# Up projection of a gated MLP: two running sums that shared one two-bank PSUM tile get a tile each

## The chip, the cores and the metric

The kernel runs on one core of a Trainium2 chip. TensorE (PE) multiplies matrices and writes to PSUM, VectorE (DVE) and ScalarE (ACT) do element-wise work and read PSUM, GpSimd (POOL) and SyncE (SP) here issue DMA transfers. PSUM has eight banks of 2 KB per partition; 512 float32 numbers fill one bank. The metric is the device time of the kernel in microseconds; lower is better. Several runs are taken and their median is given.

## The reference

One encoder layer on 512 tokens of 2048 channels, in float32: a norm, an input projection, a convolution group and a neighbourhood-attention group, an output projection with residual, and then the gated MLP in which the change lies:

```python
xn = rms_norm(x, ffn_norm_g[l])
up = jnp.einsum("bsd,df->bsf", xn, w_up[l])          # 2048 -> 2 * 5632
up = depthwise_conv(up, ffn_dw_w[l], ffn_dw_b[l])    # width 3 over positions
gate, val = jnp.split(up, 2, axis=-1)
x = x + jnp.einsum("bsf,fd->bsd", jax.nn.silu(gate) * val, w_down[l])
```

A last norm follows.

## The kernel before

The work is laid out with channels on the 128 partitions and the 512 tokens along the free dimension. The up projection is done in 44 tiles (`NF`); tile `f` makes 128 gate channels and the 128 value channels that go with them, for all tokens, in `up(f, done)` (L647). `hidden` (L707) scales the result, runs the width-3 convolution (`conv3`, L694), applies the activation and multiplies; all but the last four tiles are stored to DRAM.

Each tile is a 2 x 2 block product: gate and value rows by even and odd chunks of the input channels, times even and odd chunks by the first and second half of the tokens (`H` = 256). It is computed with seven block products in place of eight, in the order `TURN` = 3, 2, 4, 5, 1, 0, 6. The combinations of the input that they need are made once and kept (`comb`, `halves`, L543). The combinations of the weights are made for each tile: some by a DMA that adds while it writes (`summed`, L603, its POOL transfer on L605), some by DVE (L615, L617).

To keep float32 accuracy, every operand is split into a high and a low part. A unit of weights (128 x 1024) is loaded to `raw` (L110), ACT makes its high part `whi` (L115), and DVE makes the rest, `wlo` (L116). `weights()` (L151) makes units three products ahead of their use; there are four buffers for each of `whi` and `wlo` and nine for `raw`. Sums by DMA are started eight products ahead.

A block product has eight steps. In `product` (L649) a step is one matmul of the high weights with 512 columns (L656; 256 columns of high input and 256 of low input) and one of the low weights with 256 columns (L659). Product 2 does it in three matmuls of 256 columns (`mm3`, L125). So a PSUM bank holds two halves that have yet to be added: `folded` (L668) copies the right half to SBUF on ACT (L669) and adds the left half on DVE (L670).

Five banks hold running sums of one tile: `pa`, `pe`, `pd_`, `pb` and `pc_`. They are allocated once, before the loop over tiles. `pa` is begun by product 3, and products 4 and 1 are added to it. Between these, `copied` (L664) copies it on ACT (L666) to other banks, from which these go on:

- after product 3: `pd_` is a copy of `pa`, to which product 5 is added; folded, it is the first token half of the gate
- after product 4: `pe` is a copy of `pa`, to which product 0 is added; folded, it is the first token half of the value, before `w` is added
- after product 1: `pb` is a copy of `pa`, to which product 6 is added; folded, it is the second token half of the gate
- `pa` itself after product 1, folded, is the second token half of the value, before `w` is added
- `pc_` takes product 2, and goes to both value halves as `w` (L677, L689)

`pd_`, `pb` and `pc_` are PSUM tiles of one bank each. `pe` and `pa` are the two banks of one PSUM tile, `ea` (tag "sc"), and one `folded(by, ea)` reads both of them after product 0. The attention stage uses the tags "sc" and "po" earlier, and the down projection uses them again afterwards (`four`, L761). Three matmuls on L645 begin `pe`, `pd_` and `pb` once, before the first tile.

The program is written in order; a scheduler gives each engine its queue, and each engine then works through its own queue in order. Waits between engines are put in from the reads and writes of tiles. `pin` keeps a matmul behind the one written before it; where the list `tight` isn't empty, the first matmul of each product and the first of each step of `mm3` are pinned. Here `tight` is filled in tile 0 after product 3, and emptied after the last tile. `done` is called after each product: it issues transfers that prepare the down projection's weights (`sum_ahead`, L175; two POOL transfers per tile, L181 and L184), and in the last tile it starts reading the stored tiles back (L748).

Of the kernel before, what the change touches and what calls it, by code (L numbers as in the profile page):

```python
# [10 lines left out]
F32 = mybir.dt.float32  # L11
# [5 lines left out]
P = 128  # L17
D = 2048
S = 512
# [51 lines left out]
def layer(ctx: ExitStack, tc: tile.TileContext, xT, w_in, w_out, w_up, w_down, par, tab, g3, out):  # L71
# [7 lines left out]
    psa = ctx.enter_context(tc.tile_pool(name="psa", bufs=1, space=bass.MemoryType.PSUM))  # L79

    @contextmanager
    def shifted(by):

        at = tc.cur_priority
        tc.cur_priority = max(at + by, 0)
        yield
        tc.cur_priority = at + (tc.cur_priority - max(at + by, 0))

    def t2(name, dt=F32):
        return tp.tile([P, S], dt, tag="t2k", name=name)  # L90
# [32 lines left out]
    tight = []  # L123

    def mm3(ps, w, wk, mh, ml, start, stop, more=False):  # L125
        hi, lo = w[:2]
        a = slice(wk * P, (wk + 1) * P)
        i = nc.tensor.matmul(ps, hi[:, a], mh, start=start, stop=False, skip_group_check=more)  # L128
        if tight:
            pin(i)  # L130
        nc.tensor.matmul(ps, hi[:, a], ml, start=False, stop=False, skip_group_check=more)  # L131
        return nc.tensor.matmul(ps, lo[:, a], mh, start=False, stop=stop, skip_group_check=more)  # L132
# [4 lines left out]
    def tick(behind):  # L137
        for todo in (steps, asteps):
            while todo:
                try:  # L140
                    with tc.issue_after(behind.ins):
                        next(todo[0])
                    break
                except StopIteration:
                    todo.pop(0)
# [5 lines left out]
    def weights():  # L151
        at = weights.at
        weights.at += 1
        for i in range(at, min(at + 1 + FAR, len(plan))):
            if i in sums:
                sums.pop(i)()
        while len(made) < min(at + 1 + AHEAD, len(plan)):
            made.append(plan[len(made)]())
        return made[at]
# [478 lines left out]
    where.append(1)  # L638
    steps.append(stats2())

    ea = psa.tile([P, 2, S], F32, tag="sc", name="pu")
    pd_, pb, pc_ = (psm.tile([P, S], F32, tag="mm", name="pu") for _ in range(3))
    pe, pa = ea[:, 0], ea[:, 1]
    for x in (pe, pd_, pb):
        nc.tensor.matmul(x, comb[3][0][:, :P], comb[3][0], start=True, stop=True)  # L645

    def up(f, done):  # L647

        def product(c, ps, more):  # L649
            hi, lo = wt = weights()  # L650
            for k in range(U):
                m, w = comb[c][k], slice(k * P, (k + 1) * P)
                if c == 2:
                    i = mm3(ps[:, :H], wt, k, m[:, :H], m[:, H:], k == 0, k == U - 1)
                    continue
                i = nc.tensor.matmul(ps, hi[:, w], m, start=k == 0 and not more, stop=False, skip_group_check=more)  # L656
                if k == 0 and tight:
                    pin(i)
                i = nc.tensor.matmul(ps[:, :H], lo[:, w], m[:, :H], start=False, stop=k == U - 1,  # L659
                                     skip_group_check=more)  # L660
            tick(i)
            done(TURN.index(c), i)

        def copied(to, ps):  # L664
            with shifted(-100):
                nc.scalar.activation(to, ps, AF.Copy)  # L666

        def folded(to, ps):  # L668
            nc.scalar.activation(to, ps[..., H:], AF.Copy)  # L669
            add(to, to, ps[..., :H])  # L670

        product(3, pa, False)
        tight[:] = [1]
        copied(pd_, pa)
        product(2, pc_, False)
        w = t2("w")[:, :H]
        nc.scalar.activation(w, pc_[:, :H], AF.Copy)  # L677
        product(4, pa, True)
        copied(pe, pa)
        product(5, pd_, True)  # L680
        g = t2("g")
        folded(g[:, :H], pd_)
        product(1, pa, True)
        copied(pb, pa)
        product(0, pe, True)
        v = t2("vl")
        by = v.rearrange("p (i t) -> p i t", i=2)
        folded(by, ea)
        add(by, by, w.unsqueeze(1).broadcast_to([P, 2, H]))  # L689
        product(6, pb, True)  # L690
        folded(g[:, H:], pb)
        return g, v
# [14 lines left out]
    def hidden(f, done):  # L707
        g, v = up(f, done)
        nc.vector.tensor_mul(g, g, rstd2[0])
        nc.vector.tensor_mul(v, v, rstd2[0])  # L710
        g, v = conv3(g, f), conv3(v, NF + f)
        nc.scalar.activation(g, g, AF.Silu)
        nc.vector.tensor_mul(g, g, v)
        if f < NF - KEEP:
            nc.sync.dma_start(hd[f], g)
        else:
            hs[f] = g
# [236 lines left out]
```

## Time and profile before

| | before |
|---|---|
| runs | 2113.78, 2118.54, 2118.21 us |
| median | 2118.21 us |
| the profiled execution's own time | 2115.08 us |
| its span, first to last instruction | 2113.1 us |
| mean granted TensorE clock | 0.996 |
| up projection's matmuls | from 706.5 to 1678.2 us |

The profile records one execution. Its page gives the busy time of each engine, the span in slices, the chain that ended last, and the costliest groups of instructions by source line. Views of the trace list who waited for whom (in order: engine, line and what it waited for, us in total, times, the longest), the instructions of a stretch in order of time (start, duration, engine, line, operation, result and operands, and in square brackets the idle time before it and what ended it), and the busy time of each engine in chosen stretches. Matmuls are pipelined, so their records overlap: the distance between two starts is what one costs. PEld is the loading of weights into the array, which overlaps matmuls. A name such as `pu` stands for all five PSUM sums of the up projection, `vl` and `g` for the value and gate results, `xc` for the input combinations.

### The profile page before, as it was taken

Reading aid. Unit: us, or ns where it says so; the run is one execution under the profiler, and the core shown is the slowest. Engines: PE = TensorE matmul, PEld = TensorE weight load, DVE = VectorE, ACT = ScalarE, POOL = GpSimd, SP = SyncE. Lnnn points to the kernel's source line nnn. Section 1 sums busy time; section 2 is a strip of 40 time slices with the busy share of each in tenths; the row PEclk is TensorE's granted clock in tenths of the full one; section 3 lists DMA queues with packets and bytes.
Section 4 is the critical chain, followed back from the end, with each engine's and each line's share of the span. In section 5 each row is a group of like instructions: output and inputs, shape, how many; then the busy total and the mean of one; then the engine's idle time right before and its main releaser. Section 6 shows DMA issues by size and latency. Waiting matters only on the chain.

```text
span 2113.1 us, 28490 instructions
## 1 busy us (share of the span) xinstructions
PE 2011.4 (95%) x10511; PEld 1682.2 (80%) x10511; DVE 1603.5 (76%) x2267; ACT 1091.4 (52%) x1680; POOL 230.1 (11%) x318
## 2 busy tenths in 40 slices
PE   8999999999999899999999999999999899999997
PEld 6888888877887787878878788787878788888886
DVE  7986796685658787877778777787877798887765
ACT  6144424456436565555555555555555554554553
POOL 0111111110011111111111111111110210000000
PEclk9999999999999999999999999999999999999999
DMA  6777677668578788888988888889886786666663
GB/s 245 178 219 190 160 189 187 181 181 266 162 180 217 175 218 241 206 246 219 236 231 225 231 213 240 227 219 253 206 238 166 262 305 215 212 211 197 190 204 116
DMA packets 141755, 446.81 MB, mean 211 GB/s; under 512 B 15920, under 2 KB 24112, under 8 KB 140208
## 3 DMA queue, kind: packets, MB, share of 16 engines
q1 hardware_dynamic: 98352, 293.99, 41.2%
q0 software_dynamic: 43264, 151.01, 34.3%
q8 instruction: 82, 1.34, 0.2%
q14 instruction: 57, 0.47, 0.1%
HBM read 426.07 MB, written 111.15 MB: 254 GB/s over the span
## 4 chain that ended last, share of the span: by engine, by line
PE 66%; issue 24%; ACT 5%; DVE 3%; DMA 2%; POOL 0%; SPq 0%; DVEq 0%; POOLq 0%; ACTq 0%
PE pu L656 21%; PE pu L659 9%; PE pj L128 6%; PE pj L132 6%; PE pj L131 6%; ACT whi L115 3%; PE po L128 3%; PE po L132 3%; PE po L131 3%; PE pu L128 2%; PE pu L131 2%; PE pu L132 2%; DVE vl L670 1%; ACT pu L666 1%; PE po L454 1%
## 5 line engine op out<-in xcount | busy, mean ns | idle before, releaser
L115 ACT ACTIVATE whi<-raw 128x1024 fp32r<-128x1024 f32 x574 | 607.1, 1058 | 886.4 <-PE pu L656 331.2
L116 DVE TENSOR_TENSOR wlo<-raw,whi 128x1024 fp32r<-128x1024 f32 x574 | 697.3, 1221 | 398.8 <-ACT whi L115 375.8
L656 PE MATMUL pu<-xc,whi 128*128 128x512 f32 x2112 | 758.8, 402 | 73.6 <-ACT pu L666 66.7
L659 PE MATMUL pu<-xc,wlo 128*128 128x256 f32 x2112 | 591.8, 280 | 0.0
L656 PEld LDWEIGHTS pu<-xc,whi 128*128 128x128 f32 x2112 | 396.7, 188 | 192.6 <-ACT pu L666 80.7
L659 PEld LDWEIGHTS pu<-xc,wlo 128*128 128x128 f32 x2112 | 398.9, 189 | 0.3 <-issue 0.2
L128 PE MATMUL pj<-xh,whi 128*128 128x512 f32 x640 | 253.4, 397 | 8.3 <-ACT whi L115 8.3
L132 PE MATMUL pj<-xh,wlo 128*128 128x512 f32 x640 | 250.4, 392 | 0.6 <-DVE wlo L116 0.6
L131 PE MATMUL pj<-xl,whi 128*128 128x512 f32 x640 | 250.7, 392 | 0.0
L776 PE MATMUL pd<-whi,ho 128*128 128x512 f32 x616 | 240.4, 391 | 1.6 <-ACT ho L737 1.6
L778 PE MATMUL pd<-whi,ho 128*128 128x512 f32 x616 | 240.2, 390 | 0.6 <-DVE ho L738 0.6
L777 PE MATMUL pd<-wlo,ho 128*128 128x512 f32 x616 | 240.4, 390 | 0.0
L328 DVE SCALAR_TENSOR_TENSOR y<-ch,prm,y 128x507 f32<-128x507 f32 (+14 forms) x240 | 169.7, 739 | 3.3
L128 PEld LDWEIGHTS pj<-xh,whi 128*128 128x128 f32 x640 | 120.7, 189 | 36.5 <-ACT whi L115 9.6
L132 PEld LDWEIGHTS pj<-xh,wlo 128*128 128x128 f32 x640 | 120.5, 188 | 27.9 <-DVE wlo L116 2.1
L131 PEld LDWEIGHTS pj<-xl,whi 128*128 128x128 f32 x640 | 120.7, 189 | 24.6 <-issue 0.7
L776 PEld LDWEIGHTS pd<-whi,ho 128*128 128x128 f32 x616 | 115.9, 188 | 26.1 <-ACT ho L737 1.9
L778 PEld LDWEIGHTS pd<-whi,ho 128*128 128x128 f32 x616 | 116.1, 188 | 25.2 <-DVE ho L738 1.1
L184 POOL DMA_DIRECT2D ws<-in_w_down x88 | 79.5, 903 | 516.5 <-DMA ws<-ws 271.6
L777 PEld LDWEIGHTS pd<-wlo,ho 128*128 128x128 f32 x616 | 116.1, 188 | 24.4 <-DVE wlo L116 0.3
L605 POOL DMA_DIRECT2D raw<-in_w_up x88 | 82.5, 937 | 486.7 <-DMA raw<-in_w_up 284.0
L128 PE MATMUL pu<-xc,whi 128*128 128x256 f32 x352 | 100.3, 285 | 0.0
(170 smaller groups left out, 2485.0 us busy)
## 6 DMA issues: line engine op xcount, KB each, us to landing
raw<-in_w_up SPq DMA_DIRECT2D x220, 512.0 KB, 5.8
ws<-in_w_down POOLq DMA_DIRECT2D x132, 512.0 KB, 6.2
raw<-in_w_up POOLq DMA_DIRECT2D x88, 512.0 KB, 8.0
raw<-ws SPq DMA_DIRECT2D x88, 512.0 KB, 4.3
raw<-in_w_in SPq DMA_DIRECT2D x80, 512.0 KB, 5.2
raw<-in_w_down SPq DMA_DIRECT2D x66, 512.0 KB, 4.4
ws<-ws POOLq DMA_DIRECT2D x44, 512.0 KB, 7.1
raw<-in_w_out SPq DMA_DIRECT2D x32, 512.0 KB, 5.0
```

The source lines that it names most:

```text
L115: i = nc.scalar.activation(hi[:, :n], raw[:, :n], AF.Copy)
L116: j = nc.vector.tensor_sub(lo[:, :n], raw[:, :n], hi[:, :n].bitcast(F32))
L128: i = nc.tensor.matmul(ps, hi[:, a], mh, start=start, stop=False, skip_group_check=more)
L131: nc.tensor.matmul(ps, hi[:, a], ml, start=False, stop=False, skip_group_check=more)
L132: return nc.tensor.matmul(ps, lo[:, a], mh, start=False, stop=stop, skip_group_check=more)
L328: nc.vector.scalar_tensor_tensor(y[:, a:b], h[:, a + j - PAD:b + j - PAD], prm[:, o + j:o + j + 1], y[:, a:b], op0=ALU.mult, op1=ALU.add)
L605: nc.gpsimd.dma_start(a[c], w_up[f, q2], accum_op=ALU.add)
L656: i = nc.tensor.matmul(ps, hi[:, w], m, start=k == 0 and not more, stop=False, skip_group_check=more)
L659: i = nc.tensor.matmul(ps[:, :H], lo[:, w], m[:, :H], start=False, stop=k == U - 1, skip_group_check=more)
L776: nc.tensor.matmul(ps[i], h[:, t], wh[:, d], start=start and not more, stop=False, skip_group_check=more)
L777: nc.tensor.matmul(ps[i], h[:, t], wl[:, d], start=False, stop=False, skip_group_check=more)
L778: return nc.tensor.matmul(ps[i], h[:, tl], wh[:, d], start=False, stop=stop, skip_group_check=more)
```

## The change

`pa` becomes the first bank of the "sc" tile, whose second bank isn't used; `pe` becomes a tile of its own, in the one-bank slot "po". The joint fold of both value halves becomes two folds of 256 columns, `pa`'s first, both still written after product 0. `tight` stays empty through tile 0: no matmul is pinned there, nor is the first one of tile 1's product 3; from tile 1's product 2 on all is pinned as before.

```diff
-    ea = psa.tile([P, 2, S], F32, tag="sc", name="pu")
+    pa = psa.tile([P, 2, S], F32, tag="sc", name="pu")[:, 0]
+    pe = psa.tile([P, S], F32, tag="po", name="pu")
     pd_, pb, pc_ = (psm.tile([P, S], F32, tag="mm", name="pu") for _ in range(3))
-    pe, pa = ea[:, 0], ea[:, 1]
     for x in (pe, pd_, pb):
         nc.tensor.matmul(x, comb[3][0][:, :P], comb[3][0], start=True, stop=True)
...
         product(3, pa, False)
-        tight[:] = [1]
+        tight[:] = [1] * (f > 0)
         copied(pd_, pa)
...
         product(0, pe, True)
         v = t2("vl")
         by = v.rearrange("p (i t) -> p i t", i=2)
-        folded(by, ea)
+        folded(by[:, 1], pa)
+        folded(by[:, 0], pe)
         add(by, by, w.unsqueeze(1).broadcast_to([P, 2, H]))
```

## The prediction

> **What bounds the kernel now.** I read the page's totals first, then the list of waits, then the timeline of one steady tile of the up projection on each engine.
>
> ```profile
> span 2113.1 us, 28490 instructions
> PE 2011.4 (95%) x10511; PEld 1682.2 (80%) x10511; DVE 1603.5 (76%) x2267; ACT 1091.4 (52%) x1680; POOL 230.1 (11%) x318
> ```
>
> TensorE (PE) works 95% of the span, so only what makes PE wait, or a new engine overtaking it, moves the end. The list of waits names two PE waits that come once per tile f (44 tiles):
>
> ```profile
> ACT whi L115 <- PE pu L656: 331.2, 218, 3.1
> PEld pu L656 <- ACT pu L666: 80.7, 44, 1.8
> PE pu L656 <- ACT pu L666: 66.7, 44, 1.5
> PEld pu L656 <- DVE vl L670: 17.4, 43, 0.4
> ```
>
> 44 waits on a PSUM copy (L666) and 43 on the value fold's add (L670). ACT's weight split (L115) in turn waits for PE, and no DMA stands in ACT's list for this stage: weights are ahead. The steady tile on PE:
>
> ```profile
> 1081.32 0.50 PE L656 MATMUL pu<-xc,whi 128*128 128x512 f32 x1 [1.52 <-ACT pu L666]
> ...
> 1093.10 0.40 PE L656 MATMUL pu<-xc,whi 128*128 128x512 f32 x1
> 1093.33 0.28 PE L659 MATMUL pu<-xc,wlo 128*128 128x256 f32 x1
> 1093.45 0.40 PE L656 MATMUL pu<-xc,whi 128*128 128x512 f32 x1
> ...
> 1095.93 0.40 PE L656 MATMUL pu<-xc,whi 128*128 128x512 f32 x1
> ...
> 1101.47 0.28 PE L659 MATMUL pu<-xc,wlo 128*128 128x256 f32 x1
> 1103.26 0.50 PE L656 MATMUL pu<-xc,whi 128*128 128x512 f32 x1 [1.52 <-ACT pu L666]
> 1103.60 0.28 PE L659 MATMUL pu<-xc,wlo 128*128 128x256 f32 x1
> ...
> 1108.90 0.28 PE L659 MATMUL pu<-xc,wlo 128*128 128x256 f32 x1
> 1109.24 0.50 PE L656 MATMUL pu<-xc,whi 128*128 128x512 f32 x1
> 1109.57 0.28 PE L659 MATMUL pu<-xc,wlo 128*128 128x256 f32 x1
> ```
>
> The two waiting rows are product 0 of neighbouring tiles: the period is 1103.26 - 1081.32 = 21.94 us. Product 4 starts at 1093.10 and product 5 at 1095.93, so a product that waits for nothing takes 2.83; within it a 512-column matmul is followed after 0.23 and a 256-column one after 0.12. Product 0 starts 1.79 after the last matmul of product 1 (1101.47), 1.67 more than 0.12, and its first matmul takes 0.34 instead of 0.23: **1.77 us lost**, 0.1 of it a restart cost. Product 3 of the next tile starts at 1109.24, 0.34 after 1108.90, and loses 0.22 + 0.10 = **0.32 us**. Together 2.09 of 21.94.
>
> **Why PE waits there.** The other engines over the same stretch:
>
> ```profile
> 1096.98 0.58 ACT L666 ACTIVATE pu<-pu 128x512 f32<-128x512 f32 x1
> ...
> 1101.67 1.06 ACT L115 ACTIVATE whi<-raw 128x1024 fp32r<-128x1024 f32 x1 [1.50 <-PE pu L656]
> 1102.63 0.58 ACT L666 ACTIVATE pu<-pu 128x512 f32<-128x512 f32 x1
> ...
> 1107.23 0.58 ACT L669 ACTIVATE vl<-pu 128x512 f32<-128x512 f32 x1
> ```
> ```profile
> 1104.01 1.23 DVE L615 TENSOR_TENSOR raw<-raw 128x1024 f32<-128x1024 f32 x1
> 1107.36 1.23 DVE L116 TENSOR_TENSOR wlo<-raw,whi 128x1024 fp32r<-128x1024 f32 x1 [2.12 <-ACT whi L115]
> 1108.50 0.68 DVE L670 TENSOR_TENSOR vl<-vl,pu 128x512 f32<-128x512 f32 x1
> ...
> 1111.17 0.68 DVE L710 TENSOR_TENSOR vl<-vl,rstd 128x512 f32<-128x512 f32 x1
> ```
>
> Product 0 adds to `pe`, which was copied out of `pa` at 1096.98 and was ready at 1097.56. It starts only when the next copy (`pb` out of `pa`, 1102.63 to 1103.21) has ended. That copy neither reads nor writes `pe`; it reads the other bank of the same tile. Product 5, whose `pd_` is a tile of its own, starts at 1095.93, with no wait, 1.05 us before the copy of that moment (1096.98). So the wait comes from sharing a tile. ACT makes it longer because the copy stands behind a weight split (1101.67). The 0.32 us has the same root: product 3 overwrites `pa`, whose only fold is the joint one, and its add ends at 1109.18.
>
> The rule of the Trainium skill, "PSUM — Partial Sum Buffer", section "PSUM bank collisions raise a hardware error", is that different engines must be kept apart by bank and quadrant; different banks ran clean together. By it the wait guards nothing and can go; the row of product 5 agrees.
>
> **The change part by part.**
>
> *`pe` to a tile of its own (bank "po").* Removes the 1.77 us in all 44 tiles: 44 x 1.77 = 77.9 us. The copy `pb` out of `pa` stays as late as now: 1.74 us after the last matmul of product 1 starts (1101.47 to 1103.21). It is next needed by product 6, one product (2.83) after product 0's start: 2.83 + 0.12 - 1.74 = 1.2 us to spare. If that cover went, product 6 would take over the wait. Bounds: 0 (the wait is something else) to 77.9. I take 77.9, since all 44 waits name this copy.
>
> *Value halves folded singly.* The half in `pa` no longer waits for product 0. Its ACT copy can follow L666 at 1103.2 and its add can follow L615 at 1105.2, four microseconds before product 3 needs `pa`: 43 x 0.32 = 13.8 us. Bounds 0 to 13.8; I take 13.8. The cost of two small operations in place of one:
>
> ```profile
> L669 ACT ACTIVATE g<-pu x88: 361/366/374, 727.8 to 1679.9; 128x256 f32<-128x256 f32 x88
> L670 DVE TENSOR_TENSOR g<-g,pu x88: 409/414/415, 729.0 to 1681.3; 128x256 f32<-128x256 f32 x88
> ...
> L669 ACT ACTIVATE vl<-pu x44: 577/581/595, 735.1 to 1680.5; 128x512 f32<-128x512 f32 x44
> L670 DVE TENSOR_TENSOR vl<-vl,pu x44: 678/680/681, 736.4 to 1682.7; 128x512 f32<-128x512 f32 x44
> ```
>
> In this tile's view (min/median/max ns), ACT gets 2 x 366 - 581 = 151 ns more a tile and DVE 2 x 414 - 680 = 148 ns. I cost both at nothing, because the engines have room in the shorter period:
>
> ```profile
> 600.00:700.00 100.00, 99.94 (x463) 80.37 (x462) 75.54 (x137) 57.06 (x104) 13.01 (x17) 1.00 0.86 211
> ...
> 1085.30:1107.23 21.93, 20.35 (x122) 17.56 (x121) 16.93 (x20) 12.12 (x18) 3.25 (x4) 1.00 0.87 239
> ```
>
> (Columns: stretch, its length, busy time of PE, PEld, DVE, ACT, POOL, then clock, DMA share, GB/s.) DVE would have 16.93 + 0.15 = 17.08 of 21.94 - 2.09 = 19.85 us, 86%; ACT 62%. Without cover they would cost 44 x 0.15 = 6.6 us each. The first row, of the output projection, shows PE 99.94% busy at clock 1.00, so a fuller PE need not lose clock.
>
> *Order free in the first tile.* `tight` stays empty in tile 0, so its products and the first product of tile 1 aren't held behind the matmul before them. The place where that can matter:
>
> ```profile
> 713.58 0.79 PE L656 MATMUL pu<-xc,whi 128*128 128x512 f32 x1 [3.25 <-DVE xc L547]
> ```
> ```profile
> 713.50:716.00 2.50, 2.42 (x11) 2.33 (x11) 1.36 (x5) 1.93 (x6) 0.00 (x0) 0.50 0.94 140
> 716.00:718.00 2.00, 2.00 (x10) 2.00 (x10) 1.75 (x9) 1.15 (x2) 0.00 (x0) 0.50 1.08 216
> 718.00:720.00 2.00, 2.00 (x14) 2.00 (x14) 1.76 (x5) 0.00 (x0) 0.00 (x0) 0.71 0.13 32
> ```
>
> PE waits 3.25 us for the last operand of product 3. Product 2 is next, and needs the same operands only for its eighth step; seven steps of three 256-column matmuls at 0.12 are 2.5 us and could fill that wait. Bounds: a loss of 1.0 (product 2 no longer covers the copy `pd_` out of `pa`, 0.4 to 1.0 us after product 3) to a gain of 2.5 plus the slow clock that follows the wait, 4.5 us at 0.50 and 2.0 at 0.71, which is 2.25 + 0.58 = 2.8 of lost work, together 5.3. I take 2.5. By the Trainium skill's "TensorE: Matmul & The Clock Gate", section "What's actually happening", about 3.4 us of idleness halves the clock. The rows after the 3.25 us wait agree, and the steady tile's 1.52 us waits do not trigger it (clock 1.00). By that rule a filled wait keeps the clock and the first tile gives 5.3, with a total 2.8 us lower.
>
> *What comes next.* The tightest feed is product 1's summed weight: it is loaded, then a second load is added on top by POOL.
>
> ```profile
> 1091.71 1.42 SPq L110 DMA_DIRECT2D raw<-in_w_up  x2
> ```
> ```profile
> 1099.29 0.86 POOL L605 DMA_DIRECT2D raw<-in_w_up  x1 [10.12 <-DMA raw<-in_w_up]
> ```
> ```profile
> 1112.29 1.06 ACT L115 ACTIVATE whi<-raw 128x1024 fp32r<-128x1024 f32 x1 [1.86 <-issue]
> ```
>
> The load starts when DVE frees a buffer, and lands 7.6 us later; the adding transfer takes about as long, so its sum is there at about 1106.9. By the order of the weights the split at 1112.29, right after product 3, is the one that reads it: 5.4 us to spare, 3.3 in the shorter tile. So I charge nothing.
>
> *Sum.* The profiled execution took 2115.1 us, 2.0 more than its span. 2115.1 - 77.9 - 13.8 - 2.5 = 2020.9. The median of the runs (2118.2) is 3.1 above the profiled execution, so **2024 us** is my forecast for the median.
>
> **The rivals.**
>
> 1. *DMA takes part of it back.* The DMA share of 0.87 over 21.93 us is 19.1 us of packets, 96% of a 19.85 us tile. For it: in this row the queues are the fullest resource after PE. Against it: two queues overlap (a share of 1.08 stands above), and they are fed in bursts behind DVE, not late for ACT now. If packets stretch by a tenth when nothing is idle, the tile is 21.0 and the gain 44 x 0.94 = 41 us: 2118.2 - 41 - 2.5, about 2075.
>
> 2. *The change doesn't do what it says.* If product 0 waited for the copy for another reason than the tile, only 13.8 + 2.5 remain: 2102. Against it: product 5's row.
>
> 3. *Slower: the `pa` fold's add falls behind in DVE's queue.* Product 3 of the next tile waits for it. DVE's run from 1107.36 to 1111.17 is unbroken; if the scheduler placed this add last in that run, it would end 2.15 us after product 6 (1108.90 + 0.12). Product 3 would then lose about 2.25 instead of 0.32, which cancels the 1.77. The kernel is slower from 2.09 us of lateness on. Two weight subtractions (L116, 1.23 each) ahead of it as well make 2.4 more: 2118.2 + 43 x (2.25 + 2.4 - 2.09) - 2.5 = 2226. Against it: the add is ready before that run starts, with DVE idle from 1105.24 to 1107.36.
>
> 4. *The joint wait only.* If product 3 keeps its 0.32 because both folds are issued together, 2038.
>
> **How the numbers follow.** Forecast 0.70 (first-tile bounds and a run spread of a few us make its own range 2014 to 2033); rival 4 0.08; rival 1 0.14; rival 2 0.03; rival 3 0.05. The range 2014 to 2062 holds the forecast, rival 4 and the milder third of rival 1, which is 0.8 with some tail left below. A measurement tells 0.3% (6.4 us) from no change. Faster: 0.70 + 0.08 + 0.14 + 0.02 of rival 2 = 0.94; within 0.3%: 0.02, from rivals 2 and 3; slower: 0.04.
>
> **What would show it.** Right: the 44 PE waits on L666 vanish and product 0 starts 0.12 us after product 1's last matmul, with L666 running beside it; no PE wait on L670; the tile's period is 19.85; the first tile has no 3.25 us wait on L547. Wrong: PE waits on L666 now stand at product 6; ACT's L115 waits on DMA (rival 1); PE waits on L670 over 2 us (rival 3); or the period stays near 21.9 (rival 2).

## The result and the profile after

| | before | after |
|---|---|---|
| median of the runs | 2117.07 us (4 runs, 2113.78 to 2118.54) | 2020.44 us (4 runs, 2018.15 to 2021.26) |
| the profiled execution's own time | 2115.08 us | 2021.06 us |
| its span | 2113.1 us | 2019.1 us |

The ratio is 0.9544, with a 95% interval from 0.9527 to 0.9560: the kernel is 4.6% faster. The forecast was 2024 us, with a range from 2014 to 2062.

The totals of the page after, and its chain that ended last:

```profile
span 2019.1 us, 28450 instructions
## 1 busy us (share of the span) xinstructions
PE 1990.3 (99%) x10511; PEld 1682.7 (83%) x10511; DVE 1608.5 (80%) x2311; ACT 1104.1 (55%) x1724; POOL 230.2 (11%) x318
...
PE 97%; ACT 1%; DMA 1%; DVE 1%; issue 0%; SPq 0%; POOLq 0%; POOL 0%; DVEq 0%
```

PE has the same 10511 matmuls in 94.0 us less. ACT and DVE each have 44 instructions more: the single folds. Both PE waits of the up projection are gone from the list of waits. This is PE around product 0, product 6 and the next product 3 of a steady tile:

```profile
1004.77 0.28 PE L659 MATMUL pu<-xc,wlo 128*128 128x256 f32 x1
1004.88 0.40 PE L656 MATMUL pu<-xc,whi 128*128 128x512 f32 x1
...
1007.60 0.28 PE L659 MATMUL pu<-xc,wlo 128*128 128x256 f32 x1
1007.72 0.40 PE L656 MATMUL pu<-xc,whi 128*128 128x512 f32 x1
...
1010.42 0.28 PE L659 MATMUL pu<-xc,wlo 128*128 128x256 f32 x1
1010.53 0.40 PE L656 MATMUL pu<-xc,whi 128*128 128x512 f32 x1
```

Product 0 starts at 1004.88, 0.11 us after the last matmul of product 1 (1.79 before). Product 6 starts at 1007.72 and product 3 of the next tile at 1010.53, both without a gap; in the steady tiles no first matmul takes 0.50 any more. ACT in that time:

```profile
1004.97 1.06 ACT L115 ACTIVATE whi<-raw 128x1024 fp32r<-128x1024 f32 x1 [1.50 <-PE pu L656]
1005.94 0.58 ACT L666 ACTIVATE pu<-pu 128x512 f32<-128x512 f32 x1
1006.45 0.37 ACT L669 ACTIVATE vl<-pu 128x256 f32<-128x256 f32 x1
1007.92 0.39 ACT L669 ACTIVATE vl<-pu 128x256 f32<-128x256 f32 x1 [1.10 <-PE pu L659]
```

The copy still stands behind the weight split, as late as before. But now it runs beside product 0, and ends at 1006.52, 1.20 us before product 6 needs it. `pa`'s fold follows at once; `pe`'s comes when product 0 has ended. The stretch of one tile, with the columns as above (length, PE, PEld, DVE, ACT, POOL, clock, DMA share, GB/s):

```profile
1000.00:1019.85 19.85, 19.85 (x122) 17.61 (x122) 17.26 (x22) 12.42 (x19) 3.24 (x4) 1.00 0.97 254
```

PE is busy all the time. Where the 94.0 us of span came from, by the starts of products in both traces:

| part | before | after | difference |
|---|---|---|---|
| start of the span to the first product of tile 0 | 707.22 | 710.10 | +2.88 |
| from there to product 2 of tile 1 | 32.75 | 25.52 | -7.23 |
| 42 tiles, product 2 to product 2 | 42 x 21.897 | 42 x 19.840 | -86.41 |
| from the last product 2 to the down projection | 20.45 | 18.78 | -1.67 |
| down projection to the end | 433.01 | 431.44 | -1.57 |

The first row is no effect of the change. Execution e7 below does the same work there and reached the first product at 705.79; the two part between 500 and 510 us, where the clock is 0.66 and PE busy for 5.74 us in the kernel after, against 1.00 and 7.95 in e7. The last row holds a fall of the clock too: just behind the up stage, from 1680 to 1685 us, it is 0.67 in the kernel before, and the kernel after has no such fall there (1.00 from 1590 to 1600); whether that belongs to the change isn't shown. So the comparisons that follow use the length of the up stage alone, from its first product to the first matmul of the down projection (before 972.87 us, after 877.56, a gain of 95.3).

### The profile page after: what moved, and what is told of

It is laid out like the page before. It is cut to its first block, busy times and chain, and to the rows that moved or that the text cites. A ratio compares the mean times of both kernels' runs of the same rounds, so it can differ in the third digit from the quotient of the medians.

```text
span 2019.1 us, 28450 instructions
## 1 busy us (share of the span) xinstructions
PE 1990.3 (99%) x10511; PEld 1682.7 (83%) x10511; DVE 1608.5 (80%) x2311; ACT 1104.1 (55%) x1724; POOL 230.2 (11%) x318
## 4 chain that ended last, share of the span: by engine, by line
PE 97%; ACT 1%; DMA 1%; DVE 1%; issue 0%; SPq 0%; POOLq 0%; POOL 0%; DVEq 0%
PE pu L656 25%; PE pu L659 12%; PE pj L128 7%; PE pj L132 7%; PE pd L778 7%; PE pd L779 7%; PE pd L777 7%; PE pj L131 7%; PE po L128 3%; PE po L131 3%; PE po L132 3%; PE pu L128 2%; PE pu L131 2%; PE pu L132 2%; PE po L454 1%; PE sc L414 1%
## 5 line engine op out<-in xcount | busy, mean ns | idle before, releaser
L656 PE MATMUL pu<-xc,whi 128*128 128x512 f32 x2112 | 748.8, 399 | 0.0
L128 PE MATMUL pj<-xh,whi 128*128 128x512 f32 x640 | 254.4, 399 | 8.0 <-ACT whi L115 8.0
L128 PEld LDWEIGHTS pj<-xh,whi 128*128 128x128 f32 x640 | 121.3, 189 | 36.3 <-ACT whi L115 9.4
L131 PEld LDWEIGHTS pj<-xl,whi 128*128 128x128 f32 x640 | 121.2, 189 | 24.7 <-issue 0.7
L128 PE MATMUL pu<-xc,whi 128*128 128x256 f32 x352 | 99.7, 283 | 0.5 <-ACT xc L546 0.5
```

## The experiments

Each was timed against the kernel before, run again beside it (medians 2116.43 us for e1 to e4, 2117.03 for e5 to e7, 2116.77 for e8 and e9). The stage lengths come from one profiled execution each.

| kernel | median us | ratio to before, 95% | up stage us | steady tile us |
|---|---|---|---|---|
| e1, after, tile 0 pinned | 2025.97 | 0.9573 (0.9560 to 0.9586) | 882.87 | 19.84 |
| e2, before, tile 0 free | 2111.98 | 0.9981 (0.9972 to 0.9991) | 968.42 | 21.91 |
| e3, before, halves folded singly | 2169.03 | 1.0251 (1.0238 to 1.0264) | 1025.46 | 23.10 |
| e4, after, `pa`'s fold late | 2022.20 | 0.9555 (0.9541 to 0.9570) | 877.55 | 19.84 |
| e5, after, `pd_` shares instead | 2260.93 | 1.0681 (1.0660 to 1.0701) | 1099.26 | 25.20 |
| e6, before, copy ahead of the split | 2068.78 | 0.9770 (0.9752 to 0.9788) | 926.88 | 20.83 |
| e7, after, one more transfer a tile | 2018.54 | 0.9535 (0.9516 to 0.9555) | 877.57 | 19.84 |
| e8, after, two more | 2019.60 | 0.9538 (0.9522 to 0.9555) | 877.50 | 19.84 |
| e9, after, four more | 2093.92 | 0.9892 (0.9874 to 0.9910) | 954.73 | 19.84, then 19.8 to 24.7 |

### e1 and e2: what the free first tile is worth

```diff
 e1, from the kernel after
-        tight[:] = [1] * (f > 0)
+        tight[:] = [1]
 e2, from the kernel before
-        tight[:] = [1]
+        tight[:] = [1] * (f > 0)
```

> The changed kernel with tile 0 pinned as before. Theory: filling the 3.25 us wait of tile 0 is worth 5.2 us (tile 0 took 32.75 us from its first product to tile 1's product 2 before, 25.52 after, and 2.06 of the difference is what every tile gains), half of it by the clock that no longer falls. So 2020.4 + 5.2, about 2025.6 us, with the wait on L547 of about 3.2 us and a clock near 0.5 behind it back again, and a steady tile of 19.84 us. Rival: the time saved in tile 0 is lost again at its edges (the stage started 2.9 us later after the change): 2020 to 2022 us.

> The kernel before with only the first tile's order freed. Theory: 2117 - 5.2, about 2112 us, the 44 waits of product 0 on L666 unchanged and the steady tile still 21.9 us. Rival: the two parts need each other, or tile 0's gain is lost at its edges: 2116 to 2118 us.

Putting the pins back costs 882.87 - 877.56 = 5.3 us of the stage; freeing the tile alone gives 972.87 - 968.42 = 4.5 us, and 2116.43 to 2111.98 in the medians. Within a microsecond the two parts add, and the saving isn't lost at the edges. In e1, PE in tile 0, first its timeline and then its stretches:

```profile
716.07 0.80 PE L656 MATMUL pu<-xc,whi 128*128 128x512 f32 x1 [3.25 <-DVE xc L547]
```
```profile
716.00:718.50 2.50, 2.44 (x11) 2.34 (x11) 1.35 (x5) 1.92 (x6) 0.00 (x0) 0.50 0.92 197
718.50:721.00 2.50, 2.50 (x13) 2.50 (x13) 2.25 (x9) 1.15 (x2) 0.00 (x0) 0.50 0.92 178
```

and the same place in the kernel after:

```profile
716.24 0.39 PE L128 MATMUL pu<-xc,whi 128*128 128x256 f32 x1 [0.52 <-ACT xc L546]
```
```profile
716.00:718.50 2.50, 2.26 (x16) 2.13 (x17) 2.35 (x9) 2.49 (x9) 0.00 (x0) 1.00 0.95 166
718.50:721.00 2.50, 2.50 (x16) 2.18 (x15) 2.36 (x9) 1.86 (x3) 0.00 (x0) 1.00 0.96 175
```

With the pins, PE waits 3.25 us and then works at clock 0.50. Without them, product 2 (L128) fills the wait, 0.52 us is left, and the clock stays at 1.00. So the gain has two halves: the wait, and the slow clock behind it.

The pins of the later tiles do nothing here. With `tight` left empty throughout, the compiled program is the same as the kernel after, instruction for instruction, so it has no run of its own.

### e3 and e5: does the wait belong to the shared tile?

e3 is the kernel before with the new folding, `pe` and `pa` still in one tile. e5 is the kernel after with `pd_` put in `pa`'s tile; `pe` keeps its own.

```diff
 e3, from the kernel before
-        folded(by, ea)
+        folded(by[:, 1], pa)
+        folded(by[:, 0], pe)
 e5, from the kernel after
-    pa = psa.tile([P, 2, S], F32, tag="sc", name="pu")[:, 0]
+    ad = psa.tile([P, 2, S], F32, tag="sc", name="pu")
+    pd_, pa = ad[:, 0], ad[:, 1]
     pe = psa.tile([P, S], F32, tag="po", name="pu")
-    pd_, pb, pc_ = (psm.tile([P, S], F32, tag="mm", name="pu") for _ in range(3))
+    pb, pc_ = (psm.tile([P, S], F32, tag="mm", name="pu") for _ in range(2))
```

> The kernel before (pa and pe still two banks of one tile), with the value halves folded one by one. Theory: a tile is waited for as a whole. Then product 0 keeps its wait on L666 (1.77 us), both folds wait for product 0, and product 3 waits for the later of the two adds, which stands behind L617 in DVE's queue: about 1.1 us more than now. 2117 + 43 x 1.1, about 2160 us. Rival 1, the folding is what pays: near 2020 to 2040 us. Rival 2, waits go by bank: 2100 to 2104 us, product 3's wait alone gone.

> The changed kernel, but pd_ instead of pe shares pa's tile. Theory: the waits follow the shared tile. Product 5, which adds to pd_, now waits for the copy of pa to pe behind the weight split (1.77 us), product 0 does not, and product 1, which adds to pa, waits for the fold of pd_ (its add ended 2.7 us after product 1 began in the kernel before): 44 x (1.77 + 2.8) = 200 us, about 2220 us, at least 2098. Rival: the wait of before belongs to product 0 or to its place in the order, not to the shared tile: product 0 waits again, or nothing does (2020 us).

e3's PE waits in one steady tile, its DVE queue before the second of them, and ACT's copy of `pe`:

```profile
1009.86 0.49 PE L656 MATMUL pu<-xc,whi 128*128 128x512 f32 x1 [1.51 <-ACT pu L666]
1016.99 0.50 PE L656 MATMUL pu<-xc,whi 128*128 128x512 f32 x1 [1.31 <-DVE vl L670]
```
```profile
1015.05 0.41 DVE L670 TENSOR_TENSOR vl<-vl,pu 128x256 f32<-128x256 f32 x1
1015.38 1.22 DVE L617 TENSOR_TENSOR raw<-raw 128x1024 f32<-128x1024 f32 x1
1016.52 0.41 DVE L670 TENSOR_TENSOR vl<-vl,pu 128x256 f32<-128x256 f32 x1
```
```profile
1015.50 0.38 ACT L669 ACTIVATE vl<-pu 128x256 f32<-128x256 f32 x1 [1.35 <-DVE vl L670]
```

Product 3 writes `pa`, whose add (the first L670) ended at 1015.46. It starts at 1016.99, when `pe`'s add (the second, 1016.52 to 1016.93) has ended. A read of the other bank holds it: the tile is waited for as a whole. Even two reads wait for each other: ACT's copy of `pe` starts only when DVE's add of `pa` has ended (1015.46). The halves of `vl` are not the reason, since in e4 below, with a tile for each sum, the two copies into `vl` run back to back. Split folds without split tiles lose 52.6 us of the stage. This also shows rival 3 of the prediction at work: an add placed behind L617 makes the kernel slower.

e5's PE waits, in one steady tile (its line numbers are one higher):

```profile
1005.42 0.51 PE L657 MATMUL pu<-xc,whi 128*128 128x512 f32 x1 [1.51 <-ACT pu L667]
1011.13 0.50 PE L657 MATMUL pu<-xc,whi 128*128 128x512 f32 x1 [2.62 <-DVE g L671]
```

The waits went with the tile. Product 5, which had started without a wait in both kernels, now waits 1.51 us for the copy; product 1 waits 2.62 us for the fold of `pd_`; product 0 and product 3 don't wait. The time came out 41 us above the expected 2220; most of that is the clock, as told at the end.

### e6: why the wait was 1.5 us and not less

In the kernel before, the weight split that stood ahead of the copy of `pa` to `pb` in ACT's queue is made to follow it (`NS` stands for an order without a semaphore).

```diff
-        i = nc.scalar.activation(hi[:, :n], raw[:, :n], AF.Copy)
+        i = split_after(nc.scalar.activation(hi[:, :n], raw[:, :n], AF.Copy))
...
+    split_after = lambda i: (ahead and tc.add_manual_dep(i.ins, ahead.pop().ins.name, NS), i)[1]
...
-        copied(pb, pa)
+        ahead.append(copied(pb, pa))
```

> The kernel before with one order changed on ACT: the copy of pa to pb goes ahead of the weight split that stood before it. Theory: the wait of product 0 is the copy (0.58 us) plus the split ahead of it (0.97 us); without the split product 0 starts about 0.9 us earlier: 44 x 0.86 = 38 us, about 2079 us, PE's wait on L666 about 0.6 us. The joint fold may also come earlier in ACT's queue, up to 14 us more. Rival: the split only moves and product 0 waits for something else: 2117 us.

PE and ACT of e6 in a steady tile:

```profile
1001.11 0.50 PE L656 MATMUL pu<-xc,whi 128*128 128x512 f32 x1 [0.73 <-ACT pu L666]
```
```profile
1000.47 0.58 ACT L666 ACTIVATE pu<-pu 128x512 f32<-128x512 f32 x1 [1.68 <-PE pu L659]
1000.97 1.05 ACT L115 ACTIVATE whi<-raw 128x1024 fp32r<-128x1024 f32 x1
1004.23 0.60 ACT L669 ACTIVATE vl<-pu 128x512 f32<-128x512 f32 x1 [2.21 <-PE pu L659]
1004.73 1.05 ACT L115 ACTIVATE whi<-raw 128x1024 fp32r<-128x1024 f32 x1
```

The wait shrinks from 1.52 to 0.73 us, and the median falls by 48 us (2117.03 to 2068.78). Of 1.064 us per tile (21.897 - 20.833), about 0.8 is this wait; the rest is product 3's, which no longer waits, because the joint fold too now comes ahead of a weight split (1004.23). Nearly half the gain of the change (46.0 of 95.3 us of the stage) was to be had by an order on ACT alone; the rest needed the tile.

### e4: is the early fold of `pa` what frees product 3?

```diff
-        product(0, pe, True)
+        m = product(0, pe, True)
...
-        folded(by[:, 1], pa)
+        folded(by[:, 1], pa, m)     # its ACT copy waits for m, the last matmul of product 0
```

> The changed kernel, with the fold of pa held back until product 0 has ended, as the joint fold was. Theory of the prediction: product 3's 0.32 us comes back, 2020.4 + 43 x 0.32, about 2034 us. Rival: with a half-size add standing first, pa is free before product 6 ends even so, and the early fold is worth nothing: 2019 to 2022 us, no wait of PE on L670 or L673.

The stage takes 877.55 us, as in the kernel after, and the tile 19.84. ACT in a steady tile (line numbers one higher up to three higher):

```profile
1005.43 0.58 ACT L667 ACTIVATE pu<-pu 128x512 f32<-128x512 f32 x1
1007.41 0.66 ACT L670 ACTIVATE vl<-pu 128x256 f32<-128x256 f32 x2 [1.40 <-PE pu L659]
1008.13 1.06 ACT L115 ACTIVATE whi<-raw 128x1024 fp32r<-128x1024 f32 x1
```

The two copies (listed as one row, x2) wait for product 0 here, and still PE waits for neither fold: they stand ahead of the weight split, where the joint fold stood behind it. The rival holds. The early fold is worth nothing that can be measured.

### e7, e8 and e9: how near is DMA?

One, two or four POOL transfers of 512 KB, DRAM to DRAM, are added to each tile; nothing reads what they write. This is e7; e8 has two at the same place, e9 two there and two after product 4.

```diff
         if at == 3:
             sum_ahead(i)
+        if at == 6:
+            behind(nc.gpsimd.dma_start(spare[len(spent) % 8], w_down[len(spent) % NK, A11]), i)
+            spent.append(1)
```

> The changed kernel with one more DRAM to DRAM transfer of 512 KB in every tile, into a buffer that nothing reads. How near is DMA to being the bound? If its share of 0.97 is a ceiling, four POOL transfers take 54.5% of 19.84 us, so a fifth adds about 2.4 us and the tile becomes about 21.6 us: 2020 + 43 x 1.8, about 2097 us, ACT's weight split waiting on DMA. If the share counts packets that overlap, the tile stays at 19.84 us and the time within 2018 to 2026 us, with longer landing times only.

> The changed kernel with two more 512 KB transfers in every tile that nothing reads; one more left the tile at 19.84 us while the DMA share went only from 0.92 to 0.99 (850 to 950 us). If the queues are about full now, the next one shows: tile above 20.5 us, about 2050 us or more, ACT's weight split waiting on DMA. If the share is no ceiling at 0.99 either: 2015 to 2024 us.

> The same with four more transfers a tile, 2.1 MB on top of about 5 MB. Theory (DMA has a ceiling that the weight loads would feel): if the ceiling is near 389 GB/s, the highest stretch seen before, 5.0 MB read and written in 254 GB/s times 19.84 us plus 4 x 0.52 MB each read once and written once is at or over it, and the tile grows to 21 to 24 us, 2070 to 2200 us, with PE waiting for ACT or DVE and these for DMA. Rival (PE stays the bound): within 2015 to 2026 us.

With one more (e7) the tile stayed at 19.84 us and the median at 2018.54. The same 100 us in e8, then in e9:

```profile
850.00:950.00 100.00, 100.00 (x606) 88.66 (x605) 86.01 (x106) 62.22 (x91) 21.62 (x30) 1.00 1.02 305
```
```profile
850.00:950.00 100.00, 96.00 (x573) 84.82 (x572) 81.03 (x100) 58.76 (x86) 23.51 (x37) 0.98 1.04 334
```

Two more transfers fit: 305 GB/s, against 247 in the kernel after in these 100 us, and every steady tile is 19.84 us. Four don't: e9's tiles hold 19.84 us only up to about 910 us, and then take 19.8 to 24.7, at 313 to 328 GB/s in the stretches of 100 us from 900 on. From 800 to 900 the queues carried 328 GB/s with no loss yet. Four transfers at the old pace would need about 353 GB/s, an estimate from 247 and four times 0.52 MB in 19.84 us. No figure of GB/s is a limit by itself: right behind the up stage the kernel after moves 394 GB/s with PE busy throughout (1590 to 1620), in another mix of transfers. What gives way first in e9 is seen in its list of waits from 740 to 1640 us, and in one tile on ACT and PE:

```profile
ACT whi L115 <- DMA raw<-in_w_up: 165.0, 45, 6.0
...
PE pu L656 <- ACT pu L666: 51.1, 31, 3.2
```
```profile
915.40 1.06 ACT L115 ACTIVATE whi<-raw 128x1024 fp32r<-128x1024 f32 x1 [4.92 <-DMA raw<-in_w_up]
916.37 0.58 ACT L666 ACTIVATE pu<-pu 128x512 f32<-128x512 f32 x1
```
```profile
917.00 0.50 PE L656 MATMUL pu<-xc,whi 128*128 128x512 f32 x1 [2.11 <-ACT pu L666]
```

A late load holds a weight split; the PSUM copy is queued behind that split; and PE waits for the copy. In this list PE never waits for the weights themselves. e9's stage is 77 us longer than that of the kernel after (954.73 against 877.56): 51.1 us are these waits, and about 22 are 13 falls of the clock behind them, 3.4 us each at 0.50.

## Why the prediction was right

*`pe` to its own tile, 77.9 us, and product 3, 13.8 us.* Together 91.7 us, from a tile of 21.94 us that loses 2.09. The mean tile went from 21.897 to 19.840, so it lost 2.06. The cause was the shared tile: e3 kept the tile and kept the wait, e5 moved the sharing and moved the wait. That the copy would stay late and product 6 would have 1.2 us to spare is what ACT and PE show (1006.52 and 1007.72).

The size of the second term fits, its mechanism was not the one predicted; that the number held is luck. The prediction laid it to the early fold of `pa`. e4 holds that fold back and loses nothing; e6 frees product 3 with the joint fold in place. What cost 0.32 us was that the joint fold stood behind a weight split on ACT. Why the scheduler put the single folds ahead of that split is not shown.

*The two small operations, cost 0.* PE is busy for 19.85 of 19.85 us while DVE does 17.26 and ACT 12.42; the folds are hidden.

*The first tile, 2.5 us.* This is the term that was mis-sized: it measured 5.3 us (e1). The value taken counted the wait that product 2 fills, and not the clock. The bounds had it, as 2.8 us of lost work at the slow clock. The sentence that drew on the Trainium skill's "TensorE: Matmul & The Clock Gate", section "What's actually happening", gave 5.3 by the rule that idleness halves the clock, and the trace agrees with that much: clock 1.00 after, 0.50 in e1. It does not agree with the 3.4 us of idleness: in the kernel before the clock fell 2.0 us into the wait of 3.25 (1.00 from 710.4 to 712.0, 0.66 in the next microsecond). The last section shows what it went by.

*Rival 1, DMA, 0.14.* It did not come about. Transfers do take longer when the tile is shorter, as the two pages list their median time to landing; before:

```profile
raw<-in_w_up SPq DMA_DIRECT2D x220, 512.0 KB, 5.8
...
raw<-in_w_up POOLq DMA_DIRECT2D x88, 512.0 KB, 8.0
```

and after:

```profile
raw<-in_w_up SPq DMA_DIRECT2D x220, 512.0 KB, 7.3
...
raw<-in_w_up POOLq DMA_DIRECT2D x88, 512.0 KB, 9.4
```

In e3 and e5, whose tiles are longer, the first of these is 5.1 and 4.5 us. But the lead of the loads covers that: in the kernel after, ACT never waits for DMA in the steady tiles. The share of 0.97 was no ceiling; e8 carried 1.02 with no loss. e9 shows that the rival is a real one further on.

*Rival 2* falls with e5. *Rival 3* is what e3 shows, with one other operation ahead of the add, and there because the tile was shared; in the kernel after the adds are early. *Rival 4* is out: product 3 starts without a gap, in e4 too, where both folds come together.

*The sum.* The stage became 95.3 us shorter, against 94.2 in the sum: 5.3 for the first tile (2.5), and so 90.0 for the two waits (91.7). The medians differ by 96.6 (2117.07 - 2020.44). The 2 us more than the sum lie within the spread of the runs.

## What to carry to other kernels

Look for a wait that names a reader of another bank of the same PSUM tile: sums with different lives want tiles of their own, and splitting only the readers can make it worse. When an engine on the path waits for a small operation, look at what is queued ahead of that operation on its own engine; here another order on ACT alone was worth nearly half of what the whole change gave. To judge a resource that looks nearly full, load it further and see which wait appears first.

## What the runs showed of the hardware that was not expected

A PE wait shorter than the 3.25 us of tile 0 can halve the clock. e5 waits 2.62 us in every steady tile. Its tiles, product 2 to product 2, are of two kinds: 22 of 43 take 24.2 to 24.7 us, the other 21 take 25.6 to 27.1. In one of the longer ones the wait ended at 858.95, and soon after:

```profile
857.00:859.00 2.00, 0.05 (x1) 0.05 (x1) 1.55 (x2) 0.58 (x2) 0.17 (x1) 1.00 0.96 229
859.00:860.00 1.00, 1.00 (x6) 0.87 (x7) 0.00 (x0) 0.00 (x0) 0.00 (x0) 0.99 1.06 221
860.00:862.00 2.00, 2.00 (x8) 1.71 (x7) 0.00 (x0) 0.00 (x0) 0.00 (x0) 0.50 1.09 371
862.00:864.00 2.00, 2.00 (x10) 1.72 (x9) 0.00 (x0) 0.60 (x1) 0.00 (x0) 0.65 0.58 236
```

The clock is still 1.00 in the wait and 0.50 in full work a microsecond later; by the last row it has come back after some 3.4 us. One such fall costs about 1.5 us a tile, 32 us in the whole stage, which is most of what e5 took beyond its expected time. The waits of 1.52 us in the kernel before never did it.

What decides is shown by the record of the granted clock that each trace holds. In each of the eleven traces (before, after, e1 to e9) the falls lie whole multiples of 3.413 us apart; e5 has the most, 24. So the stretch from 695 to 1880 us of every trace can be cut into steps of 3.413 us, 3749 of them at full clock, and in each step the time be counted in which PE's records show no matmul (their ends are modelled). The clock fell at the end of 44 steps, and each of these had more than 1.84 us without a matmul; none of the other 3705 had more. Two steps of e5, just short of that and just beyond it:

```profile
1361.75:1365.16 3.41, 1.56 (x10) 1.11 (x8) 0.83 (x1) 1.33 (x2) 0.84 (x2) 1.00 0.94 298
1511.93:1515.34 3.41, 1.53 (x9) 1.35 (x10) 1.56 (x2) 0.50 (x2) 0.09 (x1) 1.00 1.00 223
```

PE is busy for 1.56 us of the first, and the clock stayed; for 1.53 us of the second, and it fell at 1515.35. In these traces, then, a wait of 1.52 us cannot reach the limit alone, wherever it lies. One of 2.62 us reaches it when more than 1.84 us of it lie in one step; 21 of e5's 43 tiles lost the clock, and the others kept it.
